# Another order of the tiles in one pool, and a fill tile: the same instructions at other SBUF addresses

## The chip, the cores and the metric

The kernel runs on one core of one Trainium2 chip. The metric is the time of one execution on the device in microseconds (us); shorter is better. A time is the median of several executions.

## The reference

Two decoder layers (`DEPTH = 2`) over 256 tokens of width 1024, in float32:

```python
def swiglu(x, w_gate, w_up, w_down):
    return (jax.nn.silu(x @ w_gate) * (x @ w_up)) @ w_down

for l in range(DEPTH):
    f = swiglu(x, ffn_w_gate[l, 0], ffn_w_up[l, 0], ffn_w_down[l, 0])      # 1024 -> 2816 -> 1024
    x = layer_norm(ALPHA * x + 0.5 * f, ln_g[l, 0], ln_b[l, 0])
    z = x @ w_in[l]                                                        # 1024 -> 2304
    y_a = mixer_spatial_gating(z[..., :512], ...)
    y_b = mixer_short_conv(z[..., 512:1280], ...)
    y_c = mixer_rglru(z[..., 1280:], ...)                                  # conv, gates, a scan over time
    y = jnp.concatenate([y_a, y_b, y_c], axis=-1) @ w_out[l]
    x = layer_norm(ALPHA * x + y, ln_g[l, 1], ln_b[l, 1])
    f = swiglu(x, ffn_w_gate[l, 1], ffn_w_up[l, 1], ffn_w_down[l, 1])
    x = layer_norm(ALPHA * x + 0.5 * f, ln_g[l, 2], ln_b[l, 2])
```

## The kernel before

All weights lie in HBM as 320 blocks of 128 partitions x 1024 float32 (512 KB). `stream` (it calls `dma` and `split`) loads a block into one of six tiles `raw0` to `raw5`; ScalarE (ACT) copies it to `wh`, rounded to the matmul's float32r type (L278), and VectorE (DVE) writes the rest, raw minus wh, to `wl` (L284). `wh` and `wl` have twelve tiles each. Activations are kept in two parts in the same way: `xTh`, `xTl` (the layer's input, transposed), `hTh`, `hTl` (the hidden layer of an FFN) and `yTh`, `yTl` (what the mixer's groups give). Each product is three matmuls, high x high, high x low and low x high, all of them recorded at L308.

A matmul has a stationary operand of 128 columns, loaded by a weight load (PEld), and a moving operand that streams through it. In the rows a matmul reads `bank<-moving,stationary`. There are three kinds of float32r matmul:

- `sub_T` (and `first_unit`): `xTh` or `xTl` moves, 256 columns; a 128-column piece of `wh` or `wl` is stationary. It makes the gate and up products of the FFNs and most of the mixer's input projection.
- `down` (through `mm_nat`): a half block of `wh` or `wl` moves, 512 columns; 128 columns of `hTh`, `hTl` (FFN) or `yTh`, `yTl` (the mixer's output projection) are stationary. At the very end of the kernel the second half is cut in two of 256.
- `nat_step`: `wh` or `wl` moves, 512 or 256 columns, and `xTh`, `xTl` are stationary. It is the first piece of three FFNs and of both mixers.

Besides, there are plain float32 matmuls: transposes (L312, `ident` moves), the RG-LRU gates (`xr` moves, `wa` and `wi` are stationary) and the spatial gate (`vn` moves, `wT` is stationary).

Every operation is recorded first (`Program.add`), with a cost and its dependences on cells of buffers. `Program.issue` then issues them engine by engine from those costs and due times. Neither looks at an address. Addresses come later, when tiles are taken from pools: the buffers made with no pool name (`cbufs`) go into the pool `const`, one behind the other in the order in which `buf` was called, and each of the phases (`x0`, four FFNs `f00` to `f11`, two mixers `m0`, `m1`) opens a pool behind it and closes it before the next. A tile takes its bytes in a partition, rounded up to 32.

In the order of the calls `const` holds, in bytes of a partition: `xTh` and `xTl` 8192 each, `xn0` and `xn1` 4096 each, `ident` 512, `prm` 304, `der` 96, `mhalf` 4, `quarter` 4, `gB` and `bB` 4096 each, six `raw`, twelve `wh`, twelve `wl` of 4096 each, and 14 tiles of 4 to 72 bytes (`st`, `mv`, `ve`, `rs`, `sp`). The pool begins on a multiple of 128 bytes.

Of the kernel before, what the change touches and what calls it, by code (L numbers as in the profile page):

```python
# [10 lines left out]
F32 = mybir.dt.float32  # L11
# [5 lines left out]
P = 128  # L17
# [8 lines left out]

RING = 12
RAW = 6
TAIL = 6
TR0, TR1 = 4, 6  # L30
TAIL_OUT = 6
# [229 lines left out]
def build(tc, a):  # L261
# [59 lines left out]
    cbufs, opened = [], {}  # L321

    def buf(name, shape, dtype=F32, pool=None, **kw):
        b = Buf(name, shape, dtype, phase=opened.get(pool), **kw)
        (cbufs if pool is None else phases[pool]).append(b)
        return b
# [30 lines left out]
    bB = buf("bB", (D,), grain=512)  # L357
    raw = [buf(f"raw{i}", (D,), grain=256) for i in range(RAW)]
    wh = [buf(f"wh{i}", (D,), F32R, grain=256) for i in range(RING)]
# [9 lines left out]
    def bank(*shape):  # L369
        b = bank_fifo.pop(0)  # L370
        return b.alias(shape) if shape else b
# [8 lines left out]
    def stream(upto, part=None):  # L380
        assert upto <= pos["blk"] + RING
        while loaded["n"] < min(upto, nblk):
            i = loaded["n"]
            r, h, l = raw[i % RAW], wh[i % RING], wl[i % RING]
            sl = slice(0, D) if part is None else slice(part * 512, part * 512 + 512)
# [80 lines left out]
    def down(lh, ll, n, tail, scale, eps, last, nxt):  # L466
        halves = [slice(0, 512), slice(512, D)]
        cols = [halves, [slice(0, 512), slice(512, 768), slice(768, D)] if last else halves]
        accs = [[(bank(), cs) for cs in cols[h]] for h in range(2)]
        blks = []  # L470

        def step(f, h, c):
            hs = slice(h * P, (h + 1) * P)
            acc, cs = accs[h][c]
            i = blks[f] % RING
            mm_nat(acc[:cs.stop - cs.start], lh[f, hs], ll[f, hs], wh[i][cs], wl[i][cs], f == 0, f == n - 1)

        for f in range(n - tail):
            blks += take(1)
            for h in range(2):  # L480
                for c in range(len(cols[h])):
                    step(f, h, c)
        ln0 = LN(0, accs[0], scale, eps, last)
        blks += take(tail)
        for c in range(2):
            for f in range(n - tail, n):
                step(f, 0, c)
            ln0.stats(c)
        ln0.finish()
        ln1 = LN(1, accs[1], scale, eps, last)  # L490
        end = tail if last else 2
        for j, f in enumerate(range(n - tail, n - end)):
            for c in range(len(cols[1])):
                step(f, 1, c)
            if not last and j >= tail - 4:
                ln0.trans(j - (tail - 4))
        for c in range(len(cols[1])):
            for f in range(n - end, n):
                step(f, 1, c)
            ln1.stats(c)  # L500
        ln1.finish()
        if nxt:
            load_gb(*nxt)
        return ln1


    def ffn(layer, i, ln_prev, nxt, mid=None):
# [35 lines left out]
        for j, (kind, c0, n) in enumerate(units):  # L543
# [21 lines left out]
            if mid and j == 3:  # L565
                mid()
        return down(hTh, hTl, NF, TAIL, 4.0 * ALPHA, 16.0 * EPS, last, nxt)

# [242 lines left out]
    b = bank()  # L811
# [20 lines left out]
    with st:  # L832
        cpool = st.enter_context(tc.tile_pool(name="const", bufs=1))
        ppool = st.enter_context(tc.tile_pool(name="psum", bufs=1, space=PSUM))
        for b in cbufs:
            b.tile = (ppool if b.psum else cpool).tile([P, *b.shape], b.dtype, name=b.name)
        with tc.manual_schedule():
            pr.issue()
            while stack:
                stack.pop().close()  # L840
# [82 lines left out]
```

## Time and profile before

| | |
|---|---|
| median of 3 executions | 926.17 us (925.65 to 927.35) |
| the profiled execution | 927.02 us |
| its span, first to last instruction | 925.3 us |
| granted TensorE clock over the span | 0.998 of full |
| PE (matmul) busy | 914.5 us, 99% |
| PEld (weight load) busy | 846.2 us, 91% |
| DVE busy / ACT busy | 601.1 us, 65% / 436.5 us, 47% |

The span is what the profile's rows cover; 1.7 us of the profiled execution lie around it. Matmuls overlap in the rows, since each ends after the next has begun, so a matmul's price in a stream is the distance from its start to the start of the next, and not its duration. The columns of a timeline are start in us, duration in us, engine, line, operation, output<-inputs, partitions x columns, how many were merged, and in brackets the idle time ahead and what ended it.

### The profile page before, as it was taken

The page shows a single profiled execution, that of the slowest core. Times are in us where ns is not written, and L with a number is a line of the kernel's source. Part 1 is how long each engine was busy: PE and PEld are TensorE (multiplying, and loading weights), DVE is VectorE, ACT ScalarE, POOL GpSimd, SP SyncE. Part 2 cuts the span into 40 slices and gives each one's busy share as a digit, 9 for nine tenths or more (in the row PEclk, how much of TensorE's full clock was granted, in tenths as well). Part 3 has the DMA queues.
Part 4 walks back from the last instruction along what each step waited for, and adds up shares of the span by engine and source line. Part 5 has one row for each costly group of instructions (what it writes and reads, how often), then busy time and mean ns, then how long its engine had stood idle before and what let it go on. Part 6 is the DMA issues. An engine that isn't in the chain of part 4 may idle for free.

```text
span 925.3 us, 15553 instructions
## 1 busy us (share of the span) xinstructions
PE 914.5 (99%) x6348; PEld 846.2 (91%) x6348; DVE 601.1 (65%) x813; ACT 436.5 (47%) x549; POOL 19.7 (2%) x33
## 2 busy tenths in 40 slices
PE   9999999999999999999999999999999999999996
PEld 8999998889989999988899999888898899999885
DVE  6896664497888665654696666545978876566415
ACT  6564443267645444443344444443575454444410
POOL 0000000011000000000000000000100000000000
PEclk9999999999999999999999999999999999999999
DMA  8996566466358555555375655553863585665401
GB/s 309 343 330 205 188 189 189 160 225 234 111 163 282 191 185 185 194 190 183 121 264 207 185 187 196 186 183 118 309 201 96 183 276 182 186 192 192 138 1 45
DMA packets 51910, 178.25 MB, mean 193 GB/s; under 512 B 6144, under 2 KB 7936, under 8 KB 51840
## 3 DMA queue, kind: packets, MB, share of 16 engines
q1 hardware_dynamic: 51840, 177.28, 58.1%
q8 instruction: 49, 0.80, 0.3%
q14 instruction: 21, 0.17, 0.0%
HBM read 176.20 MB, written 1.05 MB: 192 GB/s over the span
## 4 chain that ended last, share of the span: by engine, by line
PE 96%; DVE 2%; ACT 1%; DMA 1%; SPq 0%; issue 0%; DVEq 0%; ACTq 0%
PE bank L308 94%; PE bank L312 1%; DMA raw<-w 1%; DVE xr L704 1%; SPq L318 0%; DVE ib L284 0%; DVE xn L296 0%; ACT L278 0%; ACT e L278 0%; DVE ra L284 0%; DVE yTl L284 0%; ACT wh L278 0%; ACT cc L278 0%; DVE wl L284 0%; DVE cc L284 0%
## 5 line engine op out<-in xcount | busy, mean ns | idle before, releaser
L284 DVE TENSOR_TENSOR wl<-raw,wh 128x1024 fp32r<-128x1024 f32 (+1 forms) x320 | 386.3, 1210 | 240.4 <-ACT wh L278 239.4
L278 ACT ACTIVATE wh<-raw 128x1024 fp32r<-128x1024 f32 (+1 forms) x320 | 333.6, 1049 | 393.0 <-PE bank L308 279.3
L308 PE MATMUL bank<-xTh,wh 128*128 128x256 f32 x1456 | 408.7, 281 | 0.8 <-ACT wh L278 0.8
L308 PE MATMUL bank<-xTh,wl 128*128 128x256 f32 x1456 | 406.7, 279 | 0.2 <-DVE wl L284 0.2
L308 PE MATMUL bank<-xTl,wh 128*128 128x256 f32 x1456 | 406.6, 279 | 0.0
L308 PEld LDWEIGHTS bank<-xTh,wh 128*128 128x128 f32 x1456 | 273.9, 188 | 1.9 <-ACT wh L278 1.0
L308 PEld LDWEIGHTS bank<-xTh,wl 128*128 128x128 f32 x1456 | 274.1, 188 | 0.4 <-DVE wl L284 0.4
L308 PEld LDWEIGHTS bank<-xTl,wh 128*128 128x128 f32 x1456 | 274.2, 188 | 0.2
L308 PE MATMUL bank<-wh,hTh 128*128 128x512 f32 (+1 forms) x374 | 143.1, 383 | 0.0
L308 PE MATMUL bank<-wl,hTh 128*128 128x512 f32 (+1 forms) x374 | 143.0, 382 | 0.0
L308 PE MATMUL bank<-wh,hTl 128*128 128x512 f32 (+1 forms) x374 | 142.8, 382 | 0.0
L308 PEld LDWEIGHTS bank<-wh,hTl 128*128 128x128 f32 x374 | 70.3, 188 | 14.8
L308 PEld LDWEIGHTS bank<-wh,hTh 128*128 128x128 f32 x374 | 70.3, 188 | 14.7
L308 PEld LDWEIGHTS bank<-wl,hTh 128*128 128x128 f32 x374 | 70.4, 188 | 14.5
L308 PE MATMUL bank<-wh,xTh 128*128 128x256 f32 (+1 forms) x160 | 54.5, 341 | 0.0
L308 PE MATMUL bank<-wl,xTh 128*128 128x256 f32 (+1 forms) x160 | 54.4, 341 | 0.0
L308 PE MATMUL bank<-wh,xTl 128*128 128x512 f32 (+1 forms) x160 | 53.7, 338 | 0.0
L296 DVE SCALAR_TENSOR_TENSOR xn<-xn,bank 128x512 f32<-128x512 f32 (+1 forms) x25 | 16.6, 662 | 44.0 <-PE bank L308 44.0
L284 DVE TENSOR_TENSOR hh<-th,bank 128x512 f32<-128x512 f32 (+1 forms) x42 | 27.5, 655 | 18.7 <-PE bank L308 18.6
L284 POOL TENSOR_TENSOR rs<-ve,mhalf 128x1 f32<-128x1 f32 x16 | 14.7, 920 | 899.8 <-DVE ve L291 899.8
L308 PEld LDWEIGHTS bank<-wl,xTh 128*128 128x128 f32 x160 | 30.1, 188 | 3.9
L308 PEld LDWEIGHTS bank<-wh,xTh 128*128 128x128 f32 x160 | 30.1, 188 | 3.8
(95 smaller groups left out, 526.7 us busy)
## 6 DMA issues: line engine op xcount, KB each, us to landing
raw<-w SPq DMA_DIRECT2D x312, 512.0 KB, 4.2
gB<-ln_g SPq DMA_DIRECT2D x6, 512.0 KB, 6.2
bB<-ln_b SPq DMA_DIRECT2D x6, 512.0 KB, 6.3
raw<-w SPq DMA_DIRECT2D x8, 256.0 KB, 5.2
x0t<-xT SPq DMA_DIRECT2D x8, 128.0 KB, 5.2
xn<-x SPq DMA_DIRECT2D x2, 512.0 KB, 6.0
out<-xn SPq DMA_DIRECT2D x3, 256.0 KB, 2.1
wT<-sgu_wT SPq DMA_DIRECT2D x2, 256.0 KB, 6.3
```

Of the source, the lines that this page charges most:

```text
L278: pr.add("A", cost, views(in_, scale, bias), [out], lambda: A.activation(out=ap(out), in_=ap(in_), func=func, scale=ap(scale), bias=ap(bias)))
L284: pr.add(eng, cost, [in0, in1], [out], lambda: e.tensor_tensor(out=ap(out), in0=ap(in0), in1=ap(in1, F32 if as32 else None), op=op))
L296: pr.add("V", cost, views(in0, s, in1), [out], lambda: V.scalar_tensor_tensor(out=ap(out), in0=ap(in0), scalar=ap(s), in1=ap(in1), op0=op0 ...
L308: pr.add("T", cost, [lhsT, rhs], [out], lambda: T.matmul(out=ap(out), lhsT=ap(lhsT), rhs=ap(rhs), start=start, stop=stop))
L312: pr.add("T", 109.0, [in_, ident.all], [out], lambda: T.transpose(out=ap(out), in_=ap(in_), identity=ap(ident.all)))
L704: pr.add("V", 336.0, [ra[k, :], ib[k, :]], [xr[k, :]], lambda k=k: V.tensor_tensor_scan(out=ap(xr[k, :]), data0=ap(ra[k, :]), data1=ap(ib[ ...
```

## The change

The pool `const` is filled in another order: buffers whose size is a multiple of 64 elements (256 bytes) come first, in their old order, and the others (`prm`, `der`, `mhalf`, `quarter` and the 14 small tiles) come behind them. After these a tile `fill`, which no instruction uses, brings the pool's end to a multiple of 256 bytes from its beginning. Phase pools begin behind it.

```diff
--- before.py
+++ after.py
@@ -26,6 +26,7 @@
 
 RING = 12
 RAW = 6
+LINE = 64
 TAIL = 6
 TR0, TR1 = 4, 6
 TAIL_OUT = 6
@@ -832,8 +833,13 @@
     with st:
         cpool = st.enter_context(tc.tile_pool(name="const", bufs=1))
         ppool = st.enter_context(tc.tile_pool(name="psum", bufs=1, space=PSUM))
-        for b in cbufs:
+
+        small = [b for b in cbufs if not b.psum and math.prod(b.shape) % LINE]
+        for b in sorted(cbufs, key=lambda b: b in small):
             b.tile = (ppool if b.psum else cpool).tile([P, *b.shape], b.dtype, name=b.name)
+        taken = sum(-(-math.prod(b.shape) // 8) * 8 for b in small)
+        if taken % LINE:
+            cpool.tile([P, LINE - taken % LINE], F32, name="fill")
         with tc.manual_schedule():
             pr.issue()
             while stack:
```

Addresses of the tiles, as bytes past a multiple of 128:

| tiles | before | after |
|---|---|---|
| `xTh`, `xTl`, `xn`, `ident` | 0 | 0 |
| `gB`, `bB`, `raw`, `wh`, `wl` | 96 | 0 |
| `x0t`, `zero`, `hTh`, `hTl`, `th`, `hh`, `thn`, `hn`, `wT`, `wa`, `wi`, `sg`, `sb` | 32 | 0 |
| in the mixer, behind the 16 bytes of `bs`: `yTh`, `yTl`, `un`, `vn`, `gT`, `xr`, `ra`, `ib`, `e2`, `cc`, `cy` | 64 | 32 |

The first line holds since all tiles ahead of them are multiples of 128 bytes. The second: 304, 96, 4 and 4 bytes, rounded up to 32, are 320 + 96 + 32 + 32 = 480, which is 3 x 128 + 96. The third: the 14 small tiles take another 2 x 96 + 12 x 32 = 576 = 4 x 128 + 64, and 96 + 64 = 160 = 128 + 32. The fourth: `bs` takes 32 more. A slice of `raw`, `wh` or `wl` that the kernel uses begins at a multiple of 128 columns, 512 bytes, so all slices keep the offset of their tile.

No instruction is added, removed or moved: on every engine the issue order of the changed kernel reads row for row like that of the kernel before, with the same buffers in the same slots.

## Rows read from the trace of the kernel before

**Rows 1.** The page: busy time of each engine; granted clock in 40 slices.
```profile
PE 914.5 (99%) x6348; PEld 846.2 (91%) x6348; DVE 601.1 (65%) x813; ACT 436.5 (47%) x549; POOL 19.7 (2%) x33
...
PEclk9999999999999999999999999999999999999999
```

**Rows 2.** The page: the chain that ended last, its share by engine.
```profile
PE 96%; DVE 2%; ACT 1%; DMA 1%; SPq 0%; issue 0%; DVEq 0%; ACTq 0%
```

**Rows 3.** Groups of instructions by shape, PE: count | busy us, mean ns | idle before.
```profile
L308 PE MATMUL bank<-xTh,wh 128*128 128x256 f32 x1456 | 408.7, 281 | 0.8 <-ACT wh L278 0.8
...
L308 PE MATMUL bank<-wl,hTh 128*128 128x512 f32 x330 | 130.8, 396 | 0.0
...
L308 PE MATMUL bank<-wh,xTh 128*128 128x512 f32 x80 | 31.6, 395 | 0.0
L308 PE MATMUL bank<-wh,yTh 128*128 128x512 f32 x64 | 25.6, 400 | 0.0
...
L308 PE MATMUL bank<-wh,xTh 128*128 128x256 f32 x80 | 22.9, 286 | 0.0
...
L308 PE MATMUL bank<-wh,hTh 128*128 128x256 f32 x44 | 12.3, 280 | 0.0
```

**Rows 4.** Timeline, PE, 320 to 330 us (sub_T): first and last of 88.
```profile
319.81 0.28 PE L308 MATMUL bank<-xTl,wh 128*128 128x256 f32 x1
...
329.96 0.28 PE L308 MATMUL bank<-xTl,wh 128*128 128x256 f32 x1
```

**Rows 5.** Timeline, PE, 420 to 430 us (down of an FFN): first and last of 45.
```profile
419.71 0.39 PE L308 MATMUL bank<-wl,hTh 128*128 128x512 f32 x1
...
429.98 0.39 PE L308 MATMUL bank<-wh,hTh 128*128 128x512 f32 x1
```

**Rows 6.** Timeline, PE (nat_step, 256 columns): first of 24, and the matmul behind them.
```profile
208.28 0.28 PE L308 MATMUL bank<-wh,xTh 128*128 128x256 f32 x1
...
211.12 0.28 PE L308 MATMUL bank<-xTh,wh 128*128 128x256 f32 x1
```

**Rows 7.** Timeline, PE (end of the last down): first and last of 36.
```profile
913.42 0.28 PE L308 MATMUL bank<-wh,hTh 128*128 128x256 f32 x1
...
917.54 0.28 PE L308 MATMUL bank<-wh,hTl 128*128 128x256 f32 x1
```

**Rows 8.** Timeline, PE (down of a mixer): first and last of 57.
```profile
254.72 0.40 PE L308 MATMUL bank<-wl,yTh 128*128 128x512 f32 x1
...
267.84 0.40 PE L308 MATMUL bank<-wh,yTh 128*128 128x512 f32 x1
```

**Rows 9.** Timeline, PE: an RG-LRU gate's float32 products.
```profile
222.77 0.59 PE L308 MATMUL bank<-xr,wa 128*128 128x256 f32 x2
223.20 0.59 PE L308 MATMUL bank<-xr,wi 128*128 128x256 f32 x2
```

**Rows 10.** The transposes: duration ns least/median/most, first and last start.
```profile
L312 PE MATMUL bank<-ident,xn x80: 270/272/273, 188.5 to 739.5; 128*128 128x128 f32 x80
L312 PE MATMUL bank<-ident,hn x18: 271/272/273, 295.6 to 760.8; 128*128 128x128 f32 x18
```

**Rows 11.** Groups of instructions by shape, PEld (weight loads).
```profile
L308 PEld LDWEIGHTS bank<-xTl,wh 128*128 128x128 f32 x1456 | 274.2, 188 | 0.2
...
L308 PEld LDWEIGHTS bank<-wh,hTl 128*128 128x128 f32 x374 | 70.3, 188 | 14.8
...
L308 PEld LDWEIGHTS bank<-wh,xTl 128*128 128x128 f32 x160 | 30.1, 188 | 3.6
...
L308 PEld LDWEIGHTS bank<-wh,yTl 128*128 128x128 f32 x64 | 12.1, 188 | 4.6 <-DVE yTl L284 1.9
```

**Rows 12.** Timeline, PE, 9 to 13 us: the two waits for a weight block.
```profile
11.29 0.38 PE L308 MATMUL bank<-xTh,wh 128*128 128x256 f32 x1 [0.83 <-ACT wh L278]
...
12.02 0.38 PE L308 MATMUL bank<-xTh,wl 128*128 128x256 f32 x1 [0.23 <-DVE wl L284]
```

**Rows 13.** Groups of instructions by shape, DVE.
```profile
L284 DVE TENSOR_TENSOR hTl<-hh,hTh 128x256 fp32r<-128x256 f32 x5 | 2.1, 418 | 0.0
...
L284 DVE TENSOR_TENSOR yTl<-cc,yTh 128x256 fp32r<-128x256 f32 x4 | 1.6, 411 | 0.0
```

## The prediction

> **What bounds the kernel now.** I read the page first. TensorE is busy 99% of the span and its clock is granted in full in every slice, while VectorE and ScalarE stand at 65% and 47% [rows 1]. The chain that ended last says the same from the other side: 96% of it is PE [rows 2]. So the time is the number of matmuls times the distance between their starts, plus about 4% of the span in which PE stands aside (the first weights, the end of each mixer, the last layer norm).
>
> Next come the kinds of matmul and their counts. The groups by shape give one line for each of the three products, so a count in [rows 3] is taken three times: 4368 matmuls in which xTh or xTl moves 256 columns, 990 + 240 + 192 = 1422 in which wh or wl moves 512, and 240 + 132 = 372 in which they move 256. The mean durations there are not prices, since matmuls overlap. The price is the distance between starts, from the first and last row of a stretch without a gap:
>
> - sub_T: 10.15 us over 87 distances, 116.7 ns [rows 4].
> - down of an FFN: 10.27 over 44, 233.4 ns [rows 5].
> - nat_step with 256 columns: 2.84 over 24, 118.3 ns [rows 6].
> - the last down's 256 columns: 4.12 over 35, 117.7 ns [rows 7].
> - down of a mixer: 13.12 over 56, 234.3 ns [rows 8].
>
> For nat_step with 512 columns I take 233.4 too. The sum is 4368 x 116.7 + 1230 x 233.4 + 192 x 234.3 + 240 x 118.3 + 132 x 117.7 = 509.7 + 287.1 + 45.0 + 28.4 + 15.5 = 885.7 us, 96% of the 925.3 us span: the prices cover what the chain gives to PE.
>
> **What offset the prices belong to.** This is the core of the forecast, and it needs the table of offsets. In sub_T the moving operand already begins at 0 past a multiple of 128 bytes, and its stationary operand at 96. In down and nat_step the moving operand begins at 96, its stationary one at 32 (hTh), 64 (yTh) or 0 (xTh). By column, sub_T pays 116.7 / 256 = 0.456 ns and down of an FFN 233.4 / 512 = 0.456 ns. At 2.4 GHz one column in a cycle would be 0.417 ns, so both pay 9% over that, and they pay the same 9%. An operand that is on a multiple of 128 does no better in the stream than one that is not. Weight loads tell the same of the stationary side: 188 ns from wh (96), hTl (32), xTl (0) and yTl (64) alike [rows 11].
>
> What is left as a trace of the offset is small. Set against sub_T's 116.7, nat_step pays 118.3 - 116.7 = 1.6 ns more and the last down 1.0 ns more; the mixer's down pays 234.3 - 233.4 = 0.9 ns over the FFN's.
>
> **The change, part by part.**
>
> 1. *The moving operands wh and wl go from 96 to 0.* If the small surplus is the offset's, it goes: 240 x 1.6 = 0.38 us, 132 x 1.0 = 0.13, 192 x 0.9 = 0.17, together 0.7 us. The other bound below is nothing, if the surplus has another cause. I take 0.7, as the surplus stands in just the kinds in which wh or wl moves. The 1230 wide matmuls are at sub_T's price by column and I give them nothing.
>
> Here a rule of the Trainium skill speaks against even that. "SBUF — State Buffer", section "Door 1: The DMA port swizzle", says that SBUF has lines of 16 bytes, and that a penalty falls where an access crosses to a new one. Offsets of 96, 64, 32 and 0 are all multiples of 16, so by that rule no matmul would change and this term would be 0 instead of 0.7 us. By the distances, the trace agrees for the wide matmuls, and not clearly for the narrow ones.
>
> 2. *The stationary operands move too* (wh from 96 to 0, hTh from 32 to 0, yTh from 64 to 32). Loads last 188 ns at all four offsets [rows 11], so nothing.
>
> 3. *xr and vn, the moving operands of the float32 products, go from 64 to 32*, not to a multiple of 128: a mixer's bs still shifts all behind it. Two passes of xr through wa are 0.43 us apart from those through wi, 215 ns each [rows 9]; the 32 of them take 6.9 us in all. The trace has no offset of 32 for them; the transposes, plain float32 as well, show 272 ns with the stationary operand at 0 (xn) and at 32 (hn) [rows 10]. I take nothing.
>
> 4. *VectorE and ScalarE work at other offsets.* They are off the chain but for its 3%, about 28 us [rows 2]. The nearest pair is one VectorE subtraction of 256 columns with its operands at 32 and at 64: 418 against 411 ns [rows 13], 1.7%. The mixer's tiles go from 64 to 32, so at worst 28 x 1.7% = 0.5 us slower; most of those 28 us lie on tiles that don't go that way, and I take 0.2.
>
> 5. *Loads land at other offsets.* PE waits for a weight block only at the head, 0.83 and 0.23 us [rows 12]; behind it the transfers are hidden by the ring of twelve blocks. So this is worth 1.1 us at most if the first loads come earlier, and I put the same as a bound on the other side. I take nothing.
>
> 6. *The order of issue* is the same, and fill costs no instruction: nothing.
>
> Sum: -0.7 + 0.2 = -0.5 us. The profiled execution took 927.02 us, so its like would take 926.5; it stood 0.85 over the median of the runs, and off that median, 926.17, I get **925.7 us**.
>
> **The rivals.** What a measurement of this kernel can tell from no change is about 0.2%, 1.9 us, so the forecast is "no difference".
>
> *A, only together.* No float32r matmul of the trace has both operands on a multiple of 128: one of them is always wh or wl, at 96. The 9% might be the price of that one operand, as stream in down and as weight load in sub_T. What a stream without surplus costs, the float32 gates bound: a record of theirs with 256 columns takes 215 ns, which is 516 cycles of 2.4 GHz or two cycles for each column and 4 more [rows 9]; so 512 columns at one cycle each would take about 215 ns, and 256 about 108. If down and nat_step fall to that, 1422 x 18.4 = 26.2 us go, and the 372 narrow ones bring 0.5 more by falling to sub_T's price: 899 us. If sub_T falls as well, to 108, another 4368 x 8.7 = 38.0 and 372 x 8.7 = 3.2 go: 858 us. For it: 0.456 is not 0.417, and something must be the cause. Against it: a weight load and a stream would have to pay the same share to the third digit by chance, and the loads' 188 ns know no offset.
>
> [...]
>
> *B, slower: the two reads meet.* With both operands at 0 past 128 the stream and the weight load would touch the same part of a line at the same time. The price is bounded by the largest surplus that an offset shows here, nat_step's 1.6 ns: on 4368 + 1422 + 372 matmuls 9.9 us, so 935.6 us. It decides as soon as it costs 0.4 ns in each, which makes 2.4 us. Against it: the transposes with both operands at 0 (ident, xn) last 272 ns as do those with 0 and 32 [rows 10].
>
> *C, small things add up*: the head gains its 1.1 us and the surplus is somewhat larger than I count, about 923.9 us; or the head loses and the chain's 0.5 us is met in full, about 928.
>
> **How the numbers follow.** The forecast has 0.80. Rival A has 0.07 (0.05 for the wide matmuls alone, 0.02 for all), B 0.05; C beyond 0.2% has 0.06 on the fast side and 0.02 on the slow. So faster 0.13, same 0.80, slower 0.07. The range holds the forecast and most of C: downwards the surplus, the head's 1.1 and the spread of the runs (0.5 below the median), 926.17 - 0.7 - 1.1 - 0.5 = 923.9; upwards no gain, 0.5 for the chain and the spread (1.2 above), 927.9. A and B lie outside with 0.12.
>
> **What would show it right or wrong.** Right: the distance between starts stays at 116.7 in sub_T and 233.4 in down of an FFN, falls to 116.7 in nat_step and in the last down and to 233.4 in the mixer's down; weight loads stay at 188 ns; the waits at the head stay near 0.8 and 0.2 us. Rival A would show as about 215 ns in down, B as more than 117 ns in sub_T. The step most likely to fail is the comparison by column: it takes sub_T's price for that of its stream, while its weight load could hide a faster one.

## The result: slower by 0.66%, and the profile after

| | before | after |
|---|---|---|
| median | 925.91 us (925.43 to 927.35) | 932.29 us (932.10 to 932.54) |
| profiled execution, its span | 927.02, 925.3 us | 932.1, 930.4 us |

The ratio is 1.0066, with an interval of 1.0049 to 1.0084. The forecast was 925.7 us with a range up to 927.9, so the time is outside it on the slow side.

The page of the changed kernel has the other engines at the loads of [rows 1]; PE and PEld are busy longer. The chain that ended last is 96% PE, as in [rows 2].

```profile
PE 920.7 (99%) x6348; PEld 859.8 (92%) x6348; DVE 601.0 (65%) x813; ACT 436.5 (47%) x549; POOL 19.7 (2%) x33
...
PEclk9999999999999999999999999999999999999999
```

VectorE, ScalarE and the granted clock are as before. What changed is the distance between the starts of matmuls. The timeline of the changed kernel, PE, first and last row of six stretches (the last three of a nat_step with 512 columns, and the first row behind them; 24 of nat_step with 256 columns, and the first behind them; 57 of a mixer's down; 86 of sub_T; 46 of an FFN's down; 36 of the last down):

```profile
207.19 0.39 PE L309 MATMUL bank<-wh,xTh 128*128 128x512 f32 x1
...
207.87 0.28 PE L309 MATMUL bank<-wh,xTh 128*128 128x256 f32 x1
...
210.75 0.28 PE L309 MATMUL bank<-xTh,wh 128*128 128x256 f32 x1
...
254.76 0.40 PE L309 MATMUL bank<-wh,yTh 128*128 128x512 f32 x1
...
267.82 0.40 PE L309 MATMUL bank<-wh,yTl 128*128 128x512 f32 x1
...
319.79 0.28 PE L309 MATMUL bank<-xTl,wh 128*128 128x256 f32 x1
...
329.99 0.28 PE L309 MATMUL bank<-xTh,wl 128*128 128x256 f32 x1
...
419.62 0.39 PE L309 MATMUL bank<-wh,hTl 128*128 128x512 f32 x1
...
429.82 0.39 PE L309 MATMUL bank<-wh,hTl 128*128 128x512 f32 x1
...
918.42 0.28 PE L309 MATMUL bank<-wh,hTh 128*128 128x256 f32 x1
...
922.62 0.28 PE L309 MATMUL bank<-wh,hTl 128*128 128x256 f32 x1
```

| kind | before, ns | after, ns | count | change, us |
|---|---|---|---|---|
| sub_T, 256 columns | 116.7 [rows 4] | 10.20 / 85 = 120.0 | 4368 | +14.4 |
| down of an FFN, 512 | 233.4 [rows 5] | 10.20 / 45 = 226.7 | 990 | -6.6 |
| nat_step, 512 | 233.4 (taken) | 0.68 / 3 = 226.7 | 240 | -1.6 |
| nat_step, 256 | 118.3 [rows 6] | 2.88 / 24 = 120.0 | 240 | +0.4 |
| last down, 256 | 117.7 [rows 7] | 4.20 / 35 = 120.0 | 132 | +0.3 |
| down of a mixer, 512 | 234.3 [rows 8] | 13.06 / 56 = 233.2 | 192 | -0.2 |

The sum is +6.7 us; the medians differ by 6.4. The spans differ by 5.1 only, since the profiled execution of before lost time at its head, where it waited 0.83 + 0.23 us for its first blocks [rows 12] and that of after did not: the 101st matmul of the trace starts at 18.43 us before and at 16.74 after. Both traces hold the same 6348 matmuls in the same order, so the distances can also be compared one by one. Behind the 101st they sum to +6.8 us: +14.0 in sub_T, -5.8 in the FFN's down, -1.4 in the wide nat_step, -0.5 in the mixer's down (0.4 of it in two longer gaps), +0.5 in the narrow ones of nat_step and the last down. So the change did two things of opposite sign. The 1230 wide matmuls in which both operands now begin on a multiple of 128 became 2.9% faster, and the 4740 narrow ones 1.4% to 2.8% slower.

In cycles of 2.4 GHz the new prices are round: 120.0 ns is 288 = 256 + 32 and 226.7 ns is 544 = 512 + 32. For these two widths that is 32 cycles for each matmul and none that grows with the columns. Before, 116.7 ns was 280 = 256 x 35/32 and 233.4 was 560 = 512 x 35/32.

Weight loads were no guide, as they last about the same as in [rows 11]. The groups of PEld in the changed kernel:

```profile
L309 PEld LDWEIGHTS bank<-xTl,wh 128*128 128x128 f32 x1456 | 279.8, 192 | 0.2
...
L309 PEld LDWEIGHTS bank<-wh,hTl 128*128 128x128 f32 x374 | 70.4, 188 | 13.0
```

### The profile page after: what moved, and what is told of

It reads as the page before. It is cut to its first block, busy times and chain, and to the rows that moved or that the text cites. A ratio compares the mean times of both kernels' runs of the same rounds, so it can differ in the third digit from the quotient of the medians.

```text
span 930.4 us, 15553 instructions
## 1 busy us (share of the span) xinstructions
PE 920.7 (99%) x6348; PEld 859.8 (92%) x6348; DVE 601.0 (65%) x813; ACT 436.5 (47%) x549; POOL 19.7 (2%) x33
## 4 chain that ended last, share of the span: by engine, by line
PE 96%; DVE 2%; ACT 1%; DMA 0%; issue 0%; SPq 0%; DVEq 0%; ACTq 0%
PE bank L309 95%; PE bank L313 1%; DVE xr L705 1%; DMA raw<-w 0%; DVE ib L285 0%; DVE xn L297 0%; ACT L279 0%; ACT e L279 0%; DVE ra L285 0%; DVE yTl L285 0%; SPq L319 0%; ACT wh L279 0%; ACT cc L279 0%; DVE wl L285 0%; DVE cc L285 0%
## 5 line engine op out<-in xcount | busy, mean ns | idle before, releaser
L309 PE MATMUL bank<-xTh,wh 128*128 128x256 f32 x1456 | 414.2, 285 | 0.3 <-ACT xTh L279 0.3
L309 PE MATMUL bank<-xTh,wl 128*128 128x256 f32 x1456 | 412.7, 284 | 0.1
L309 PE MATMUL bank<-xTl,wh 128*128 128x256 f32 x1456 | 412.4, 283 | 0.0
L309 PEld LDWEIGHTS bank<-xTh,wh 128*128 128x128 f32 x1456 | 279.6, 192 | 1.1 <-ACT xTh L279 0.9
L309 PEld LDWEIGHTS bank<-xTh,wl 128*128 128x128 f32 x1456 | 279.8, 192 | 0.3 <-DVE wl L285 0.3
L309 PEld LDWEIGHTS bank<-xTl,wh 128*128 128x128 f32 x1456 | 279.8, 192 | 0.2
```

What stands on the lines that cost most here:

```text
L309: pr.add("T", cost, [lhsT, rhs], [out], lambda: T.matmul(out=ap(out), lhsT=ap(lhsT), rhs=ap(rhs), start=start, stop=stop))
```

## The experiments

Two theories came first. **R**: the price hangs on the distance from the start of the moving operand to that of the stationary one. **Z**: it hangs on an operand's own start on a multiple of 128. Below, L is the start of the stationary operand minus that of the moving one, modulo 256 bytes; that the circle has 256 bytes and not 128 is a result of the third and the fifth run. In these terms:

| kernel | sub_T | nat_step | down, FFN | down, mixer |
|---|---|---|---|---|
| before | 224 | 32 | 64 | 96 |
| after | 0 | 0 | 0 | 32 |

**One operand back by 32: e1_x_at_32.** On the changed kernel:

```diff
         for b in sorted(cbufs, key=lambda b: b in small):
+            if b is xTh:
+                cpool.tile([P, 8], F32, name="lead")
+            if b is xn[0]:
+                cpool.tile([P, 24], F32, name="back")
```

> The changed kernel, with xTh and xTl alone 32 bytes later (wh, wl and hTh stay on multiples of 128). Theory R (what counts is where the two operands of a float32r matmul stand against each other: equal offsets past 128 cost 32 cycles for each matmul, unequal ones 3 cycles for each 32 columns): sub_T goes from 120.0 ns back to 116.7, 4368 x 3.3 = 14.6 us less, nat_step's 240 wide matmuls go from 226.7 to 233.4, 1.6 us more, its narrow ones lose 0.4; down stays at 226.7: about 919 us against 932.3 of the changed kernel and 925.9 of the kernel before. Theory Z (what counts is each operand by itself: a weight load from a multiple of 128 is slow, a stream from one is fast): wh and wl still stand at 0, so sub_T stays at 120.0, down at 226.7, and the time at about 932.

It took 926.45 us, ratio 1.0002 (0.9992 to 1.0011). The timeline of this run, sub_T, first and last of 87 rows in one stage and of 87 in another:

```profile
319.82 0.28 PE L309 MATMUL bank<-xTh,wh 128*128 128x256 f32 x1
...
329.91 0.28 PE L309 MATMUL bank<-xTh,wl 128*128 128x256 f32 x1
...
499.75 0.28 PE L309 MATMUL bank<-xTh,wl 128*128 128x256 f32 x1
...
509.95 0.28 PE L309 MATMUL bank<-xTl,wh 128*128 128x256 f32 x1
```

10.09 / 86 = 117.3 ns and 10.20 / 86 = 118.6. The 120.0 goes, and down stays at 226.7; but sub_T does not return to 116.7, so 919 is missed by 7 us. The starts of xTh and wh are 32 apart as before in a circle of 128, and not in one of 256 (L is 96, not 224).

**Both operands by 32: e2_all_32_later.** On the changed kernel, ahead of the loop:

```diff
+        cpool.tile([P, 8], F32, name="lead")
```

> The changed kernel with every tile 32 bytes later: no operand of a float32r matmul begins on a multiple of 128, and each stands against the other as in the changed kernel. Theory R: sub_T 120.0 ns, down of an FFN 226.7, down of a mixer 233.4, about 932 us, as the changed kernel. Theory Z: with no operand at 0 it is as before, sub_T 116.7 and down 233.4, about 926 us.

It took 933.04 us, ratio 1.0073 (1.0057 to 1.009). The timeline of this run, sub_T, first and last of 85 rows:

```profile
319.83 0.28 PE L309 MATMUL bank<-xTh,wh 128*128 128x256 f32 x1
...
329.91 0.28 PE L309 MATMUL bank<-xTh,wh 128*128 128x256 f32 x1
```

sub_T has 10.08 / 84 = 120.0 ns and down 226.7, as after, though now no operand of theirs begins on a multiple of 128. Z falls: for these two it is the distance and not the place.

**Down alone: e3_before_h_at_96.** On the kernel before, behind the loop over the buffers:

```diff
+        cpool.tile([P, 16], F32, name="shift")
```

> The kernel before, with the phase pools 64 bytes later: hTh and hTl at 96 past a multiple of 128, as wh and wl are; yTh at 0; xTh at 0 and wh at 96 as before. Theory R: down of an FFN goes from 233.4 to 226.7 ns, 990 x 6.7 = 6.6 us less, the last down's 132 narrow ones go to 120.0, 0.3 more; sub_T stays at 116.7, down of a mixer near 234: about 919.6 us against 925.9. Theory Z: the stream still begins at 96, nothing changes, about 926 us.

It took 925.4 us, ratio 0.9989 (0.9979 to 0.9998). The timeline, down of an FFN, first and last of 45 rows:

```profile
419.64 0.39 PE L308 MATMUL bank<-wh,hTl 128*128 128x512 f32 x1
...
429.86 0.40 PE L308 MATMUL bank<-wl,hTh 128*128 128x512 f32 x1
```

10.22 / 44 = 232.3 ns, not 226.7: equal starts modulo 128 bring 1.1 of the 6.7 ns when they are 128 apart modulo 256. R with a circle of 128 falls.

**The price by itself: e4_offsets_alone, e5_offsets_mod_256.** Both leave the whole computation out; their core is

```python
for i in range(48):
    T.matmul(out=b[:m, :cols], lhsT=stat[n][:, o:o + m], rhs=mov[:, moff:moff + cols], start=i == 0, stop=i == 47)
```

> Leaves the whole computation out: 48 float32r matmuls a group, back to back, with one moving operand at a multiple of 128 and the stationary one 0, 4, 8, 16, 32, 64 or 96 bytes past one (384, 128 columns, 64 stationary columns, a moving operand 32 bytes on, and bfloat16 beside it). Theory R: 512 columns take 226.7 ns at offset 0 and about 233.4 at all others, 256 columns 120.0 at 0 and 116.7 to 118 at the others, 384 columns 416 cycles or 173.3 ns at 0 and 175 elsewhere; with the moving operand 32 bytes on, offset 32 is the equal one. Theory Z: offsets of the stationary operand alone change the short ones, and 512 columns take 226.7 ns at all of them, since the stream begins on a multiple of 128. If only whole lines of 16 bytes counted, 4 and 8 would read like 0.

> Leaves the whole computation out: groups of 48 float32r matmuls, back to back, the moving operand fixed and the stationary one L bytes past it in a circle of 256 bytes, L from 0 to 252. Theory R256 (the place of the two operands against each other counts, in a circle of 256 and not of 128 bytes): only L = 0 gives 544 cycles (226.7 ns) for 512 columns together with 288 (120.0) for 256; L = 128 does not repeat it but gives about 557 (232.4) and 285 (118.7), as the FFN's down did at L = 128; L = 224 gives 280 (116.7) for 256 columns, as sub_T of the kernel before. Theory R (a circle of 128): L = 128 reads as L = 0, 160 as 32, 224 as 96.

In e4 the stationary tiles were 640 bytes long, so that its "four", "sixteen" and "sixtyfour" stood at L = 132, 144 and 192; e5 mended that. The timeline of e5 (a stretch of 48 matmuls in a row, its name is L; its price is the start of the next row less its own, by 48, and holds the step to the next stretch):

```profile
18.23 21.93 PE L43 MATMUL bank<-mov,nought 128*128 128x512 f32 x96
...
106.86 11.36 PE L43 MATMUL bank<-mov,sixtyfour 128*128 128x512 f32 x48
118.06 11.29 PE L43 MATMUL bank<-mov,eighty 128*128 128x512 f32 x48
129.18 11.40 PE L43 MATMUL bank<-mov,ninetysix 128*128 128x512 f32 x48
140.42 11.36 PE L43 MATMUL bank<-mov,hundredtwelve 128*128 128x512 f32 x48
...
240.53 11.05 PE L43 MATMUL bank<-mov,twohundredfortyfour 128*128 128x512 f32 x48
251.42 11.36 PE L43 MATMUL bank<-mov,twohundredfortyeight 128*128 128x512 f32 x48
...
273.50 5.92 PE L43 MATMUL bank<-mov,nought 128*128 128x256 f32 x48
279.26 5.84 PE L43 MATMUL bank<-mov,four 128*128 128x256 f32 x48
284.93 5.73 PE L43 MATMUL bank<-mov,eight 128*128 128x256 f32 x48
290.50 5.76 PE L43 MATMUL bank<-mov,twelve 128*128 128x256 f32 x48
...
313.10 5.61 PE L43 MATMUL bank<-mov,sixtyfour 128*128 128x256 f32 x48
318.55 5.86 PE L43 MATMUL bank<-mov,eighty 128*128 128x256 f32 x48
...
358.58 5.60 PE L43 MATMUL bank<-mov,hundredninetytwo 128*128 128x256 f32 x48
364.02 5.76 PE L43 MATMUL bank<-mov,twohundredeight 128*128 128x256 f32 x48
369.62 5.76 PE L43 MATMUL bank<-mov,twohundredtwentyfour 128*128 128x256 f32 x48
375.23 5.92 PE L43 MATMUL bank<-mov,twohundredforty 128*128 128x256 f32 x48
380.98 5.92 PE L43 MATMUL bank<-mov,twohundredfortyfour 128*128 128x256 f32 x48
386.74 5.81 PE L43 MATMUL bank<-mov,twohundredfortyeight 128*128 128x256 f32 x48
```

With 256 columns L = 0 takes 5.76 / 48 = 120.0 ns, L = 224 takes 116.9, L = 8 takes 116.0, and L = 64 and 192 take 113.5 and 113.3. With 512 columns the 96 matmuls at L = 0 last from 18.23 to 40.00, where the next stretch begins: 21.77 / 96 = 226.8 ns, the price after. L = 64 takes 11.20 / 48 = 233.3 and L = 96 takes 11.24 / 48 = 234.2, the prices of the FFN's and the mixer's down before. So the prices of both kernels come out of two operands and a loop of one instruction, with no stream from memory and no other engine at work.

The same run shows that the law is less simple than was expected. L = 0 is not alone: L = 244 takes 10.89 / 48 = 226.9 ns with 512 columns and 5.76 / 48 = 120.0 with 256, and L = 240 and 252 lie within 0.4 ns of that; in e4 L = 132 took 226.7 with 512 columns, but 118.6 with 256. With 256 columns L = 112, 144 and 160 take 120.0 as well, and the other distances lie between 113.3 and 118.8. With 128 columns there is one price, 110.5 ns, at L = 0, 8 and 128. In e4 384 columns take the same 173.3 ns at L = 0 and at 32, where 175 was expected at 32; and with a stationary operand of 64 columns L = 0 takes about 230 ns for 512 columns and 113.5 for 256, so the prices here belong to stationary operands of 128 columns.

A bf16 stretch in e4 knows no offset. The timeline of e4; each row holds 48 matmuls of 512 columns and 48 of 256 (one record is missing), with L = 0 first and then 160 (its name says 32; the start of its tile adds 128):

```profile
241.24 15.55 PE L49 MATMUL bank<-movh,noughth 128*128 128x512 bf16 x95
256.84 15.55 PE L49 MATMUL bank<-movh,thirtytwoh 128*128 128x512 bf16 x95
```

15.60 / 48 = 325 ns for a wide and a narrow one together, and the equal durations say the same for L = 160.

**What the law gives in the kernel: e6_x_off_by_32_of_256, e7_before_h_y_equal.** e6 is e1 with `back` of 56 floats in place of 24, so that sub_T has L = 224 and down 0. e7 is the kernel before with this, which gives down of both kinds L = 0 and leaves sub_T alone:

```diff
         bs = mbuf("bs", 4)
+        mbuf("gap", 56)
...
+        cpool.tile([P, 48], F32, name="shift")
```

> The changed kernel with xTh and xTl 32 bytes past wh and wl in a circle of 256 bytes (the first attempt at this had moved wh and wl by 128 as well, which made it 160). Theory R256: sub_T back to 116.7 ns, 4368 x 3.3 = 14.6 us less, nat_step's wide ones 1.6 us more, its narrow ones 0.4 less, down of an FFN still 226.7: about 919 us against 932.3 and 925.9. Theory R: as in that first attempt, about 926.5 us, sub_T at 117.3 to 118.7.

> The kernel before, with the phase pools 192 bytes later and a gap in the mixer, so that hTh, hTl, yTh and yTl stand where wh and wl do, at 96 past a multiple of 256 (the first attempt had them 128 apart); everything else as before. Theory R256: down of an FFN 226.7 ns (990 x 6.7 = 6.6 us less), down of a mixer 226.7 (192 x 7.7 = 1.5 less), the last down's narrow ones 120.0 (0.3 more), sub_T 116.7: about 918.5 us against 926. Theory R: hTh at 96 was there already, so about 925 us.

e6 took 920.79 us, ratio 0.9942 (0.9925 to 0.996): sub_T 116.7, down 226.7. e7 took 919.97 us, ratio 0.9929 (0.9914 to 0.9944). The timeline of e7, down of a mixer, first and last of 54 rows:

```profile
254.79 0.39 PE L308 MATMUL bank<-wl,yTh 128*128 128x512 f32 x1
...
266.80 0.39 PE L308 MATMUL bank<-wh,yTh 128*128 128x512 f32 x1
```

12.01 / 53 = 226.6 ns. Both are faster than both kernels, by the gain of the wide matmuls without the loss of the narrow.

**The cheapest distances: e8_L_64, e9_L_192, e10_L_8.** All three have L = 0 in both kinds of down (with the `gap` of e7). e8 is e6 with `lead` of 48 floats and `back` of 16, which gives sub_T L = 64; e9 has 16 and 48, which gives 192. e10 begins xTh and xTl 248 bytes into wider tiles, which gives 8:

```diff
+            if b in (xTh, xTl):
+                wide = cpool.tile([P, KD * S + 64], b.dtype, name=b.name)
+                b.tile = wide[:, 62:62 + KD * S].rearrange("p (k s) -> p k s", k=KD)
+                continue
```

> The changed kernel with xTh and xTl moved so that wh and wl stand 64 bytes past them in a circle of 256 (sub_T at L = 64, nat_step at L = 192), and a gap in the mixer, so that yTh stands where wl does (L = 0 in both downs). In the offsets run 256 columns took 272 cycles (113.3 ns) at L = 64; before, 132 narrow matmuls at L = 64 took 282.6 (117.7). R256 with the first value: sub_T 4368 x (120.0 - 113.3) = 29.3 us less than the changed kernel, the mixer's down 192 x 6.7 = 1.3 less, nat_step's wide ones 240 x 2.2 = 0.5 more: about 904 us. With the second: 4368 x 2.3 = 10 us less: about 922. If only the stretch alone can do it and not this kernel with its changing tiles, about 922 too.

> The same with wh and wl 192 bytes past xTh and xTl (sub_T at L = 192, nat_step at L = 64). 256 columns at L = 192 took 272 cycles in one offsets run and 282.6 in the other. R256 with the first: about 905 us; with the second about 923.

> The same with wh and wl 8 bytes past xTh and xTl (sub_T at L = 8, nat_step at L = 248). 256 columns at L = 8 took 277.3 cycles (115.5 ns) in both offsets runs. R256: sub_T 4368 x 4.5 = 19.5 us less than the changed kernel, the mixer's down 1.3 less, nat_step's wide ones 1.6 more, its narrow ones 0.6 less: about 912.5 us, 8 less than either of the two kernels that had L = 224 in sub_T and L = 0 in down.

e8 took **906.41 us** (905.54 to 909.74), ratio 0.9798 (0.9779 to 0.9817), the shortest of all kernels here. Its timeline, sub_T, first and last of 91 rows in one stage and of 53 in another, the earlier one first:

```profile
205.80 0.28 PE L309 MATMUL bank<-xTl,wh 128*128 128x256 f32 x1
...
211.93 0.28 PE L309 MATMUL bank<-xTh,wl 128*128 128x256 f32 x1
...
319.76 0.28 PE L309 MATMUL bank<-xTh,wh 128*128 128x256 f32 x1
...
329.96 0.28 PE L309 MATMUL bank<-xTh,wh 128*128 128x256 f32 x1
```

6.13 / 52 = 117.9 ns and 10.20 / 90 = 113.3: two prices at one distance. e9 took 921.44 us, ratio 0.9954 (0.9939 to 0.9969): there 117.8 ns stands in the stretch at 320 us, and 113.4 in another. The two runs differ in how often each price stands: of the pieces of 24 matmuls in a row within sub_T that hold no longer gap, 146 of 157 have the lower one in e8 and 10 of 158 in e9.

e10 missed by 20 us: 932.63, ratio 1.0074 (1.0058 to 1.0091). Its timeline, sub_T, first and last of 86 rows:

```profile
319.79 0.28 PE L309 MATMUL bank<-xTl,wh 128*128 128x256 f32 x1
...
329.99 0.28 PE L309 MATMUL bank<-xTh,wl 128*128 128x256 f32 x1
```

That is 10.20 / 85 = 120.0 ns, where e5 had shown 116.0.

**Two prices at one distance: e11_two_states.** The stretches of e5, each six times behind another number of matmuls of other widths; the computation is left out:

```diff
+                for kick in range(1, 7):
+                    for _ in range(kick):
+                        T.matmul(out=banks[7][:, :64 * kick], lhsT=stat["sixteen"][:, 4:132], rhs=mov[:, :64 * kick], ...)
                     group(n, 256)
```

> Leaves the whole computation out: groups of 48 float32r matmuls of 256 columns at L = 8, 64, 96, 192, 224 and 0, each six times, with one to six other short matmuls ahead of it that shift where in their cycle the two reads begin. If the price belongs to L alone, each L has one price. If the two reads can settle in more than one pattern, some L show two prices by what went ahead: 272 and 282.6 cycles at 64 and 192, 281.6 and 284.9 at 96, and 288 alone at 0.

The timeline, two neighbouring stretches with L = 64 and the matmuls between:

```profile
83.29 5.62 PE L43 MATMUL bank<-mov,sixtyfour 128*128 128x256 f32 x48
88.75 0.90 PE L50 MATMUL bank<-mov,sixteen 128*128 128x320 f32 x5
89.48 5.82 PE L43 MATMUL bank<-mov,sixtyfour 128*128 128x256 f32 x48
```

(88.75 - 83.29) / 48 = 113.8 ns; the second has a duration longer by 0.20 us, 4 ns a matmul, which makes 117.9. The same operands settle into one of two rhythms; the stretches differ only in the matmuls ahead and in the PSUM bank they write, so what ran just before seems to have a part in which. Once settled, L = 8 had one price in all six, L = 0 too, and L = 192 one as well (117.8), where two were expected. L = 96 had 117.4 or 118.8, and L = 224 had 116.7 five times and 117.8 once.

**The miss of e10: e12_changing_tiles, e13_moving_off_16.** In e12 the tiles of one or both operands change from matmul to matmul, as in the kernel; in e13 the start of each operand is set by itself (m and s in a stretch's name). The computation is left out of both:

```diff
-T.matmul(..., lhsT=stat[n][:, o:o + m], rhs=mov[:, :cols], ...)
+T.matmul(..., lhsT=stat[n][sh][:, o + sk * P:o + (sk + 1) * P], rhs=mov[kind][mh][:, mk * S:(mk + 1) * S], ...)   # e12
+T.matmul(..., lhsT=stat[n][:, so // 4:so // 4 + P], rhs=mov[n][:, mo // 4:mo // 4 + cols], ...)                   # e13
```

> Leaves the whole computation out: groups of 48 float32r matmuls of 256 columns at L = 0, 8, 64 and 224, each with the same two operands throughout, with the moving one changing as in sub_T (two tiles, eight slices), with the stationary one changing so, and with both; three times each. It asks why sub_T took 120.0 ns at L = 8 where the stretch of equal operands took 115.5. If the changing operands are the cause (addresses that agree in a circle of 256 bytes, but not in a larger one), L = 8 takes 115.5 ns with fixed operands and about 120 with one of the changing kinds, and the kind says which side. If it is another of several patterns that is reached by what went ahead, L = 8 takes 115.5 in all four kinds here and the kernel's 120.0 stays open. L = 0 at 120.0 and L = 224 at 116.7 in all kinds, L = 64 at 113.3 or 117.8.

> A kernel that leaves the whole computation out: stretches of 48 float32r matmuls of 256 and of 512 columns, the start of the moving operand (m) and of the stationary one (s) set each by itself, in bytes past a multiple of 256; a stretch's name says both. The law that the rate hangs on the difference s - m alone (mod 256) expects one price for m0s8, m120s128, m248s0, m32s40 and m8s16, 115.5 ns at 256 columns; one price, 120.0, for m64s64 and m248s248; the prices of 64 (113.3 or 117.8) for m0s64, m192s0; of 192 (113.3 or 117.8) for m0s192, m64s0; of 224 (116.7) for m0s224 and m96s64. The rival, for the miss of the run with a difference of 8 in the whole kernel: a moving operand that itself begins 8 bytes off a multiple of 16 costs by itself, so that m120s128, m248s0 and m8s16 take 120.0 and only m0s8 and m32s40 take 115.5.

In e12 nothing changed with the tiles: L = 8 took 115.6 ns in each of the four kinds, L = 0 took 120.0 and L = 224 took 116.7. L = 64 took 117.8 in all twelve stretches, which write all eight PSUM banks in turn, so a change of the bank does not change the rhythm. The timeline of e13, its second round (the bytes of a name count from the pool's beginning; the profile cuts the digits behind s; the order is m120s128, m248s0, m32s40, m8s16, m64s64):

```profile
107.80 5.92 PE L42 MATMUL bank<-mov_m120s,stat_m120s 128*128 128x256 f32 x48
113.56 5.92 PE L42 MATMUL bank<-mov_m248s,stat_m248s 128*128 128x256 f32 x48
119.32 5.72 PE L42 MATMUL bank<-mov_m32s,stat_m32s 128*128 128x256 f32 x48
124.87 5.83 PE L42 MATMUL bank<-mov_m8s,stat_m8s 128*128 128x256 f32 x48
130.54 5.92 PE L42 MATMUL bank<-mov_m64s,stat_m64s 128*128 128x256 f32 x48
```

The first four have L = 8. The two in which the moving operand begins at 120 or 248 take 5.76 / 48 = 120.0 ns, as m64s64 with L = 0 does; that at 32 takes 115.6, that at 8 takes 118.1. In e10 xTh begins 248 bytes behind the pool's beginning and wh on a multiple of 256: the second of these rows. So the law by the distance alone is not whole: a moving operand that begins 8 bytes off a multiple of 16 has prices of its own. With both operands at 248, L = 0 takes 120.0 ns with 256 columns but 233.3 with 512: the gain of the wide ones is lost there. In the rest of e13 (starts on multiples of 32, L = 64, 192 and 224 made in several ways) the prices with 256 columns are 113.8 and 117.7 ns, the two of e8; L = 224, where 116.7 was expected, takes 117.8 each time.

## Why the prediction was wrong

**The step that failed** is the comparison by column in "What offset the prices belong to". It found 0.456 ns a column in sub_T and in down, at different offsets, and concluded: "An operand that is on a multiple of 128 does no better in the stream than one that is not". The sentence itself holds (e2), but it was used for more than it says. It compared places of one operand, and the price hangs on the distance of two. sub_T at L = 224 and down at L = 64 both happen to cost 35/32 cycles a column, and no float32r pair of the kernel before stood at L = 0, so its trace could not show what the changed kernel would pay there. Equal prices at two settings bound nothing at a third: on the circle of distances L = 0 even lies between these two. The prediction called this step the one most likely to fail, but for another reason, a faster stream hidden by the weight load.

In the sum the failure sits in two terms. **Term 2** put the move of the stationary operands at nothing, because the loads last 188 ns at all offsets. In sub_T that is the only move: xTh and xTl stay where they were, wh and wl go from 96 to 0, and 4368 matmuls became 3.3 ns dearer, 14.4 us. The loads themselves did stay near 188 ns (188 to 192), so their duration does not show what the start of a stationary operand costs the stream. The other is the nothing for the wide matmuls in term 1, below.

**Rival B** had the direction: sub_T rose above its 117 ns, as it foresaw. Its price was bounded by 1.6 ns, the largest surplus in the trace, and was 3.3. It did not see that the same distance makes wide matmuls 6.7 ns faster; that its bound, 935.6 us, lies near the measured 932.3 is luck. The argument against it, that the float32 transposes have 272 ns with equal and unequal starts [rows 10], did not carry over. The transposes have 128 columns, and with 128 columns float32r has one price too (e5). The gate products, plain float32 with 256 columns, take 215 to 216 ns at L = 224 (before [rows 9]) and at L = 0 (e7): plain float32 pays nothing for equal starts where float32r does, and so with bf16 (e4). Whether the two reads really meet, as B says, no run shows; the prices by L are shown, their cause inside the chip stays open.

**Rival A** was near in form: both operands together do what neither does alone. But what went from the wide matmuls was 6.7 of the 18.4 ns, and sub_T went the other way, so it would have named the wrong sign for the kernel.

**Term 1** (-0.7 us) had about the right size in the mixer's down, 1.1 ns in place of 0.9 (L went from 96 to 32). In the narrow matmuls its sign was wrong: nat_step and the last down rose to 120.0, since their surplus was not the offset of wh but the price of L = 32 and 64. The wide matmuls of the FFN's down and of nat_step, given nothing, brought -8.2 us by the table.

**The rule of 16-byte lines** ("SBUF — State Buffer" of the Trainium skill, "Door 1: The DMA port swizzle"), as the prediction worked it out, would have left every matmul alone, all offsets being multiples of 16. The measured 120.0 against 116.7 and 226.7 against 233.4, all at such offsets, differ from that, and the measurement decides. "TensorE: Matmul & The Clock Gate" of the Trainium skill, "Back-to-back issue gap", gives N / 2.4 + 2.5 ns as the gap of a single matmul of N columns by itself with the clock warm, and says that in a stream this over-counts at large N; worked out from it, a wide and a narrow one would take an estimated 215.8 + 109.2 = 325.0 ns. The trace agrees with that estimate for a stream of bf16 matmuls (325 ns in e4) and not for float32r, where the least seen is 226.6 and 113.3.

**Right were** terms 3 to 5: DVE and ACT at 601.0 and 436.5 us, the transposes and gates unmoved, nothing at the head that belongs to the change. The waits for the first weight blocks vary between executions: none in after, e1, e2, e6 and e8; 0.37 us in e3, 0.55 in e10, 0.66 in e7, 1.01 in e9, whatever the offset of raw.

## What to carry to other kernels

In a kernel bound by float32r matmuls, work out for each kind the start of the stationary operand less that of the moving one, modulo 256 bytes, before you align anything: here equal starts were among the best for 512 columns (226.7 ns) and among the worst for 256 (120.0), where 64 bytes apart was best. One alignment for all buffers is then the wrong question; the order of the changed kernel and 480 more bytes of unused tiles (192, 64 and 224), laid between the right buffers, made this kernel 2.0% faster than it was (e8, 1.8% to 2.2% by its interval). And a rate that is equal in two places shows only that these two are equal; look for the value that the changed kernel takes and that no pair of operands in the trace has.

## What the runs showed of the hardware

- A float32r matmul with 128 stationary columns, equal starts (L = 0) and both starts on multiples of 32 costs its columns plus 32 cycles: 288 for 256, 544 for 512 (after, e2, e4, e5). L = 240, 244 and 252 cost the same or within 0.4 ns of it (e5), and L = 132 does with 512 columns (e4).
- At the other distances tried 512 columns cost 228.9 to 234.2 ns, most often 560 cycles (233.3 ns, 35/32 a column), and 256 columns cost 113.3 to 120.0 ns (e5).
- The circle is 256 bytes: 128 apart is not equal (e3).
- At L = 64 and 192 the same stretch runs at 113.3 or 117.8 ns (e5, e8, e9, e11), and at L = 224 at 116.7 or 117.8 (e11, e13). What chooses is not settled, so e8's gain is not certain for another order of instructions.
- With the moving operand 8 bytes off a multiple of 16, distance alone no longer tells the price (e13).
- bf16 matmuls of the same shapes at L = 0 and 160 (e4), and plain float32 ones of 256 columns at L = 0 and 224 (before, e7), show none of this.
